# The sums of the adaLN modulation taken over 1024 columns and 128 rows at a time instead of 512 columns and 256 rows, and spread otherwise over the FFNs of a two-layer trunk

## The chip, the core and the metric

The kernel runs on one core of a Trainium2 chip. The metric is the device time of one execution in microseconds (us). Times are compared with those of the kernel before on the same chip.

## What is computed

A trunk of two layers over 512 positions of width 1024, all in float32. Layer 0 has a short gated convolution as its mixer, layer 1 a Mamba-2 SSD mixer; each is followed by a SwiGLU FFN (1024 to 2 x 2816 and back). What matters here is the modulation: a matrix of 1024 x 12288 is multiplied by one vector, and its 12288 results are twelve vectors of 1024, three for each of the four sub-layers.

```python
mod = (jax.nn.silu(c) @ ada_w + ada_b).reshape(bsz, DEPTH, 2, 3, D_MODEL)
for i in range(DEPTH):
    shift, scale, gate = (mod[:, i, 0, k][:, None, :] for k in range(3))
    h = rmsnorm(x, norm_g[i, 0]) * (1.0 + scale) + shift
    y = short_conv_mixer(h, ...) if i == 0 else ssd_mixer(h, ...)
    x = x + gate * rmsnorm(y, norm_g[i, 1])
    shift, scale, gate = (mod[:, i, 1, k][:, None, :] for k in range(3))
    h = rmsnorm(x, norm_g[i, 2]) * (1.0 + scale) + shift
    gate_, up = jnp.split(h @ f_w_in[i], 2, axis=-1)
    x = x + gate * rmsnorm((jax.nn.silu(gate_) * up) @ f_w_out[i], norm_g[i, 3])
```

`ada_w` is 1024 x 12288 (50 MB) and is read once. Each of its numbers is used once, so it is bound to transfers and to the engine that sums, not to matrix work.

## The kernel before

**Products.** TensorE (PE) multiplies float32 operands that are split in two halves of less precision, a high and a low one. ScalarE (ACT) rounds a staged weight tile to the high half (a CAST), and VectorE (DVE) subtracts it from the tile, which leaves the low half: this pair is called a split (L230 and L231 for tiles `wst`, L616 and L617 for tiles `wsu`). SyncE (SP) issues the loads of the weights, in the order of the program; the loads that add into a tile (`wsu<-wsu`) are issued by GpSimd (POOL).

**The order.** All of it is written out by hand: each engine gets its instructions in the order in which the program's lines come, and waits in that order. Python generators let one stage's steps be taken inside another's loop (`next(madds)`, `next(late, None)`).

**The FFNs.** The first product of each FFN (h times the 5632 columns of `f_w_in`) has two parts. Some columns go through a fast scheme with seven products per block instead of eight (a Strassen-Winograd scheme): its unit `u` takes 256 columns and issues seven groups of twelve matmuls of 256 columns, P1, P5, P2, P6, P3 for unit u and P7, P4 for the unit before, in the order P1, P7, P5, P2, P4, P6, P3. `fetch` loads a unit's weights two units ahead; `split_x`, `split_z`, `split_y`, `split_s` split them (L617); `c11`, `c12`, `c22`, `c21` combine the banks of PSUM (the memory that PE writes to) into results (L668, L672, L681, L687 to L689). In even units `c12` ends with a Silu on ACT. P4 adds into the bank that `c22` reads, and so waits for it, as `P6` waits for a copy that ACT makes of its bank (`keep`, L664). The first FFN has six such units, the second more. The rest of the columns go in plain chunks of 128 columns, 24 matmuls of 512 columns each (L285 to L287), the weights split two chunks ahead. After them comes the second factor (L1310 in the first FFN), whose weights `w2x` are split at L1282.

`Values` makes the other operand of the fast scheme from h: `sums`, `four` (two subtractions, L729), and `hi` and `lo`, which split the results (ACT L709, DVE L714).

**The modulation.** The first 16 blocks of 128 columns are done at the start by PE. All the rest is summed on DVE: `ada_load` (L997 in the loop of the first layer) brings a piece of `ada_w` into a tile `ada_st`, one of three; `ada_madd` multiplies it by a column of `csil`, which is silu(c), and adds it to `ada_acc` (L125 for the first piece, L127 for the others); `ada_fold` (L140) adds up groups of 32 partitions by a transposing reduction; `ada_fin` finishes with one small matmul (L147, `ada_ps`) and small additions on DVE (L151, L156). One load is 256 rows x 512 columns, two halves of 128 rows; so two sums of 128x512 are made from it, and a vector of 1024 needs two `ada_acc` and 16 sums. `sums(n)` takes n steps, one sum each, and a new load is issued after every second one.

In the mixer of layer 0 two to four sums stand in each chunk. In the units of the first FFN there are two, one behind `c11` and one at the end of the unit; three are ahead of the units, beside `four`. In the plain chunks that follow there are three or four in each.

The last of the twelve vectors is made inside the second FFN's units by `gate_late`, called `late`. It takes one step per unit, behind `c11`: in unit 0 it issues its first load, in unit 1 the second (L2247), and from unit 2 on it makes two sums per step, and then `ada_fin`.

Of the kernel before, what the change touches and what calls it, by code (L numbers as in the profile page):

```python
# [38 lines left out]
def trunk_kernel(  # L39
# [141 lines left out]
    def ada_first(j, i, staged, cpad):  # L181


        acc = ada_p[0].tile([P, 2, P], F32, tag="acc", name="ada0", bufs=2)
# [509 lines left out]
    class Values:  # L694
# [31 lines left out]

        def four(self, b):
            vb, k, (lo, hi) = self.vb[b], self.half[b], HALVES
            dve.tensor_tensor(vb[:, :, lo], vb[:, :, hi], vb[:, :, lo], SUB)  # L729
            self.hi(3, vb[:, :, lo], k)  # L730
            self.lo(3, vb[:, :, lo], k)
# [7 lines left out]
    ada_sets = []  # L739
    for q0 in (16, 0 + 24, 8 + 24, 16 + 24, 48, 56, 64, 72, 80):  # L740
        ada_sets += [q0 * P, q0 * P + 512]
# [4 lines left out]
    with ExitStack() as ph:  # L746
# [4 lines left out]
        four = gx.tile([P, P], F32, tag="four", name="four", bufs=1)  # L751
        make_four(four)
# [103 lines left out]
        with tc.manual_schedule(engines={PE_ENGINE, mybir.EngineType.SP, mybir.EngineType.Activation,  # L856
# [126 lines left out]
            def ada_begin(n):  # L983
                quarters.extend((c0, kh) for c0 in ada_sets[:n] for kh in range(4))
# [8 lines left out]
            def ada_load():  # L993
                if quarters:
                    c0, kh = quarters.pop(0)
                    st = ada_tile()
                    dma(st, ada_w[kh * 256:(kh + 1) * 256, c0:c0 + 512].rearrange("(k p) f -> p k f", p=P))  # L997
                    ada_st.append((c0, kh, st))

            def ada_steps():  # L1000
                n = 0
                while ada_st:
                    c0, kh, st = ada_st.pop(0)
                    if kh == 0:
                        acc = ada_p[0].tile([P, 512], F32, tag="acc", name="ada_acc", bufs=2)
                        if n % 2 == 0:
                            part = gx.tile([P, 32], F32, tag="fold", name="fold", bufs=2)
                    for k in range(2):
                        ada_madd(acc, st[:, k, :], kh * 2 + k)
                        if k:  # L1010
                            ada_load()
                            if kh == 3:
                                ada_fold(acc, part[:, n % 2 * 16:n % 2 * 16 + 16])
                                if n % 2:
                                    fins.append(ada_fin(c0 - 512, part, mm_ps if len(fins) == 2 else aux_ps))
                                n += 1
                        yield
# [40 lines left out]
            madds = ada_begin(6)  # L1058
# [13 lines left out]
            for k in range(18):  # L1072
# [20 lines left out]
                for _ in range((3, 4, 3, 2, 2, 2)[i]):  # L1093
# [241 lines left out]
        with tc.manual_schedule(engines={PE_ENGINE, mybir.EngineType.SP, mybir.EngineType.Activation,  # L1335
# [6 lines left out]
            madds = ada_begin(12)  # L1342
# [34 lines left out]
            sums(1)  # L1377
            acc.append(in_chunk(more[1], h))
            part_of.sum_s(0)
            part_of.split_s(0)  # L1380
            up(2, acc[0])
            vs.four(0)
            sums(2)
# [4 lines left out]
            for u in range(UN1):  # L1388
# [9 lines left out]
                if u:  # L1398
                    un.c12(v)
                else:  # L1400
                    vs.four(1)
# [14 lines left out]
                sums(1)  # L1416
# [17 lines left out]
                sums(1)  # L1434
# [15 lines left out]
            sums(3)  # L1450
# [6 lines left out]
            sums(2)  # L1457
# [4 lines left out]
            sums(4)  # L1462
# [16 lines left out]
            for k in range(k0, last + 1):  # L1479
# [17 lines left out]
                sums(3 if j == 3 else 4)  # L1497
# [577 lines left out]
    with ExitStack() as ph:  # L2075
# [137 lines left out]
        with tc.manual_schedule(engines={PE_ENGINE, mybir.EngineType.SP, mybir.EngineType.Activation,  # L2213
# [19 lines left out]
            four = s1t[:, 8, 0:P]  # L2233
            make_four(four)

            def gate_late():

                st = [raw[:, 18 + 2 * b:20 + 2 * b, :] for b in range(2)]
                acc = s1t[:, 9:11, :].rearrange("p a b -> p (a b)")
                part = s1t[:, 8, P:P + 32]  # L2240
                quarter = [(n, kh) for n in range(2) for kh in range(4)]

                def load(i):
                    if i < len(quarter):
                        n, kh = quarter[i]
                        c0 = 88 * P + n * T
                        dma(st[i % 2], ada_w[kh * 256:(kh + 1) * 256, c0:c0 + T].rearrange("(k p) f -> p k f", p=P))  # L2247

                load(0)
                yield  # L2250
# [283 lines left out]
```

## Time and the profile before

| | |
|---|---|
| median of 3 runs | 1344.95 us (1341.88 to 1347.98) |
| the profiled execution | 1345.36 us |
| its span in the trace | 1343.5 us |
| mean granted clock of TensorE | 0.995 |
| units of the first FFN | 253.48 to 319.79 us |
| its plain chunks | 319.79 to 455.01 us |
| from there to the second factor's first matmul | 457.36 (adaLN's), 458.46 (second factor's) |
| units of the second FFN | 1044.64 to 1206.5 us |
| adaLN's loads in the first layer's stages | 88 of 512 KB, 6.2 us from issue to landing |

In the profile, a line number is one of the kernel above, and helpers such as `product` or `split` give all their instructions one line, so that places are told apart by their time in the span. `x12` behind an operation is a group of twelve such instructions in a row. A bracket `[2.22 <-ACT g L664]` at the end of a timeline's row is the time that the engine stood idle ahead of it, and the instruction that it waited for. In rows of waits, the time in all, the number of waits and the longest stand behind the colon. Engines wait in their own order: an instruction that isn't ready holds all behind it on its engine. `SPq` and `PEq` are the sequencers that issue, `PEld` the loading of weights into TensorE beside its matmuls.

### The profile page before, as it was taken

The page shows a single profiled execution, that of the slowest core. Times are in us where ns is not written, and L with a number is a line of the kernel's source. Part 1 is how long each engine was busy: PE and PEld are TensorE (multiplying, and loading weights), DVE is VectorE, ACT ScalarE, POOL GpSimd, SP SyncE. Part 2 cuts the span into 40 slices and gives each one's busy share as a digit, 9 for nine tenths or more (in the row PEclk, how much of TensorE's full clock was granted, in tenths as well). Part 3 has the DMA queues.
Part 4 walks back from the last instruction along what each step waited for, and adds up shares of the span by engine and source line. Part 5 has one row for each costly group of instructions (what it writes and reads, how often), then busy time and mean ns, then how long its engine had stood idle before and what let it go on. Part 6 is the DMA issues. An engine that isn't in the chain of part 4 may idle for free.

```text
span 1343.5 us, 19889 instructions
## 1 busy us (share of the span) xinstructions
PE 1319.2 (98%) x7653; PEld 1145.6 (85%) x7653; DVE 1065.7 (79%) x1717; ACT 662.6 (49%) x1084; POOL 99.7 (7%) x123
## 2 busy tenths in 40 slices
PE   8999999999999899999999999999999999999998
PEld 7788889898888678898888888888789999998886
DVE  5588867786787897768999898888687788876888
ACT  5323355354122366565655555554474455454665
POOL 0000000010000140000000000000001111100330
PEclk9999999999999999999999999999999999999999
DMA  9757752587798982613542434323251999868871
GB/s 304 235 185 227 253 180 56 136 232 215 248 310 265 294 145 60 176 29 119 156 136 72 138 110 141 110 94 110 94 149 44 238 242 247 211 167 289 187 135 63
DMA packets 219939, 228.54 MB, mean 170 GB/s; under 512 B 9396, under 2 KB 163908, under 8 KB 218820
## 3 DMA queue, kind: packets, MB, share of 16 engines
q1 hardware_dynamic: 201248, 187.88, 45.3%
q0 software_dynamic: 14448, 26.48, 11.4%
q10 hardware_dynamic: 4148, 12.90, 3.0%
q8 instruction: 60, 0.98, 0.3%
q14 instruction: 35, 0.29, 0.1%
HBM read 198.52 MB, written 2.24 MB: 149 GB/s over the span
## 4 chain that ended last, share of the span: by engine, by line
PE 76%; DVE 11%; DMA 7%; ACT 3%; issue 2%; SPq 2%; DVEq 0%; ACTq 0%; POOLq 0%
PE y L387 10%; PE ip L285 9%; PE ip L287 9%; PE ip L286 9%; PE sA L654 6%; PE cA L2210 4%; DMA ada_st<-in_ada_w_dram 3%; PE sC L654 3%; PE cA L1310 3%; DVE ada_acc L127 2%; DMA wsu<-wsu 2%; PE li L285 2%; PE li L287 2%; PE li L286 2%; PE li L929 1%
## 5 line engine op out<-in xcount | busy, mean ns | idle before, releaser
L285 PE MATMUL ip<-h,whl 128*128 128x512 f32 x744 | 293.7, 395 | 0.2 <-DVE cv L1036 0.2
L287 PE MATMUL ip<-h,whl 128*128 128x512 f32 x744 | 289.9, 390 | 0.0
L286 PE MATMUL ip<-h,whl 128*128 128x512 f32 x744 | 289.6, 389 | 0.0
L285 PEld LDWEIGHTS ip<-h,whl 128*128 128x128 f32 x744 | 139.7, 188 | 29.9 <-issue 1.8
L287 PEld LDWEIGHTS ip<-h,whl 128*128 128x128 f32 x744 | 139.6, 188 | 29.9 <-DVE whl L231 0.4
L286 PEld LDWEIGHTS ip<-h,whl 128*128 128x128 f32 x744 | 139.8, 188 | 28.0
L231 DVE TENSOR_TENSOR whl<-wst,whl 128x1024 fp32r<-128x1024 f32 x86 | 104.3, 1219 | 29.2 <-ACT whl L230 29.2
L654 PE MATMUL sA<-tq,whl 128*128 128x256 f32 x792 | 104.3, 285 | 7.0 <-DVE g L681 4.0
L654 PEld LDWEIGHTS sA<-tq,whl 128*128 128x128 f32 x792 | 98.6, 192 | 10.0 <-DVE g L681 5.7
L230 ACT CAST whl<-wst 128x1024 fp32r<-128x1024 f32 x86 | 89.2, 1042 | 31.0 <-DMA wst<-in_f_w_in_dram 14.7
L127 DVE SCALAR_TENSOR_TENSOR ada_acc<-ada_st,csil,ada_acc 128x512 f32<-128x512 f32 x126 | 94.4, 749 | 11.8 <-DMA ada_st<-in_ada_w_dram 9.2
L387 PE MATMUL y<-whlo,ys 128*128 128x512 f32 x384 | 89.3, 392 | 0.0
L387 PEld LDWEIGHTS y<-whlo,ys 128*128 128x128 f32 x384 | 71.7, 188 | 15.9 <-issue 0.7
L285 PE MATMUL li<-h,whl 128*128 128x256 f32 x288 | 83.2, 289 | 0.0
L287 PE MATMUL li<-h,whl 128*128 128x256 f32 x288 | 81.5, 283 | 0.0
L286 PE MATMUL li<-h,whl 128*128 128x256 f32 x288 | 81.5, 283 | 0.0
L617 DVE TENSOR_TENSOR whl<-wsu,whl 128x1024 fp32r<-128x1024 f32 x46 | 56.1, 1220 | 24.9 <-ACT whl L616 24.7
L1673 DVE SCALAR_TENSOR_TENSOR cu<-ip,cols,cu 128x511 f32<-128x511 f32 (+2 forms) x84 | 62.8, 747 | 3.9 <-ACT cu L1670 1.4
L2210 PE MATMUL cA<-whlo,ao 128*128 128x512 f32 x264 | 61.0, 390 | 0.4 <-DVE c L2447 0.2
L2210 PEld LDWEIGHTS cA<-whlo,ao 128*128 128x128 f32 x264 | 49.3, 188 | 11.5 <-ACT whlo L2175 1.2
L285 PEld LDWEIGHTS li<-h,whl 128*128 128x128 f32 x288 | 55.2, 192 | 0.0
L286 PEld LDWEIGHTS li<-h,whl 128*128 128x128 f32 x288 | 55.2, 192 | 0.0
(383 smaller groups left out, 2509.8 us busy)
## 6 DMA issues: line engine op xcount, KB each, us to landing
ada_st<-in_ada_w_dram SPq DMA_DIRECT2D x88, 512.0 KB, 6.2
wst<-in_f_w_in_dram SPq DMA_DIRECT2D x18, 1024.0 KB, 7.7
wst<-in_m_w_in_dram SPq DMA_DIRECT2D x14, 1024.0 KB, 5.4
wsu<-in_f_w_in_dram SPq DMA_DIRECT2D x24, 512.0 KB, 5.8
sg<-in_f_w_in_dram SPq DMA_DIRECT2D x44, 256.0 KB, 3.9
wsu<-in_f_w_in_dram SPq DMA_DIRECT2D x44, 256.0 KB, 4.1
wst<-in_m_w_in_dram SPq DMA_DIRECT2D x20, 512.0 KB, 5.2
wst<-in_a_w_in_dram SPq DMA_DIRECT2D x9, 1024.0 KB, 7.3
```

The costliest lines, as they stand in the source:

```text
L127: dve.scalar_tensor_tensor(acc, w, csil[:, k:k + 1], acc, MUL, ADD)
L230: later.append((lambda sw=sw, w=w: act.copy(w[:, 0, :nk, :], sw), lambda sw=sw, w=w: dve.tensor_tensor(w[:, 1, :nk, :], sw, w[:, 0, :nk, : ...
L231: lambda sw=sw, w=w: dve.tensor_tensor(w[:, 1, :nk, :], sw, w[:, 0, :nk, :].bitcast(F32), SUB)))
L285: pe.matmul(dst, w_at(w, 0, kk), a[:, 0, sl], start=start, stop=False)
L286: pe.matmul(dst, w_at(w, 0, kk), a[:, 1, sl], start=False, stop=False)
L287: pe.matmul(dst, w_at(w, 1, kk), a[:, 0, sl], start=False, stop=stop)
L387: pe.matmul(pst, a[:, al, tk], wt[:, wl, kk, :], start=k == 0 and i == 0, stop=k == K - 1 and i == 2, skip_group_check=bool(held))
L617: dve.tensor_tensor(dst[:, 1], src, dst[:, 0].bitcast(F32), SUB)
L654: pe.matmul(dst, w[:, wl, k0 + k, :], self.moving(q, k, al), skip_group_check=True, start=q in self.FIRST and k == 0 and i == 0, stop=k == ...
L1310: pe.matmul(bank[r, sub], a[:, al, q, tk], w[:, wl, q, :], start=first and k == 0, stop=False, skip_group_check=True)
L1673: dve.scalar_tensor_tensor(u[:, sft:], pst[:, :T - sft], w[3 - sft], u[:, sft:], MUL, ADD)
L2210: pe.matmul(bank[r][sub], a[:, al, q, tk], w[:, hl, q, :], start=first and k == 0, stop=last and k == 2, skip_group_check=True)
```

## The change

A load of the modulation is now 128 rows x 1024 columns, as many bytes as before, and one sum of 128x1024 is made from it. There is one `ada_acc` of 1024 columns, and a vector of 1024 needs eight sums. A step of `sums` is one such sum, with one load issued behind it. The steps are spread otherwise: 2, 2, 1, 1, 1, 1 in the mixer's chunks; none ahead of the units of the first FFN and none in its unit 0; one in each of units 1 to 5, behind `c12`; eight between the units and the loop of plain chunks (2, 3, 3, where there were 3, 2, 4 half ones), and beyond that two per chunk (three in one). Both `four` of the first FFN's `Values` come as one, `fours`, ahead of unit 0: both subtractions, then both `hi`, then both `lo`. In the second FFN `late` takes its step behind `c12` and not in unit 0; its first step, in unit 1, issues two loads, makes the first sum and issues a third load, and each further step makes one sum.

```diff
+        def fours(self):
+            lo, hi = HALVES
+            for vb in self.vb:
+                dve.tensor_tensor(vb[:, :, lo], vb[:, :, hi], vb[:, :, lo], SUB)
+            for do in (self.hi, self.lo):
+                for vb, k in zip(self.vb, self.half):
+                    do(3, vb[:, :, lo], k)
...
-        ada_sets += [q0 * P, q0 * P + 512]
+    ada_sets = [q0 * P for q0 in (16, 24, 32, 40, 48, 56, 64, 72, 80)]
...
+        ada_acc = ada_p[0].tile([P, D], F32, tag="acc", name="ada_acc", bufs=1)
...
-                    dma(st, ada_w[kh * 256:(kh + 1) * 256, c0:c0 + 512].rearrange("(k p) f -> p k f", p=P))
+                    dma(st.rearrange("p a b -> p (a b)"), ada_w[k * P:(k + 1) * P, c0:c0 + D])
...
             def ada_steps():
                 while ada_st:
...
+                    c0, k, st = ada_st.pop(0)
+                    ada_madd(ada_acc, st.rearrange("p a b -> p (a b)"), k)
+                    ada_load()
+                    if k == KD - 1:
+                        part = gx.tile([P, 32], F32, tag="fold", name="fold", bufs=2)
+                        ada_fold(ada_acc, part)
+                        fins.append(ada_fin(c0, part, mm_ps if len(fins) == 2 else aux_ps))
+                    yield
...
-                for _ in range((3, 4, 3, 2, 2, 2)[i]):
+                for _ in range((2, 2, 1, 1, 1, 1)[i]):
                     next(madds)
...
             up(1, lead_ps[3])
-            sums(1)
             acc.append(in_chunk(more[1], h))
             part_of.sum_s(0)
             part_of.split_s(0)
+            vs.fours()
             up(2, acc[0])
-            vs.four(0)
-            sums(2)
...
                 un.product(u, "P1")
                 if u:
                     un.c12(v)
+                    sums(1)
                 else:
-                    vs.four(1)
                     up(3, acc[1])
...
                 un.c11(u)
-                sums(1)
                 un.split_z(u)
...
                     un.split_s(u + 1)
-                sums(1)
...
-            sums(3)
+            sums(2)
...
-            sums(2)
+            sums(3)
...
-            sums(4)
+            sums(3)
...
-                sums(3 if j == 3 else 4)
+                sums(3 if k == k0 + 6 else 2)
...
                 load(0)
-                yield
                 load(1)
-                for i, (n, kh) in enumerate(quarter):
+                for k in range(KD):
+                    ada_madd(acc, st[k % 2], k)
+                    load(k + 2)
+                    if k == KD - 1:
+                        ada_fold(acc, part)
                     yield
...
                     c12(v)
+                    next(late, None)
...
                 c11(u)
-                next(late, None)
```

The first place is DVE's order ahead of the first FFN's unit 0 and up to its unit 0's `c11` (L668). `raw_2192` holds the operand of `four`, `tq` its low halves, `raw_2193<-ip,g` is a product of a gate and an up half of the plain chunks ahead. Before:

```order
L637 TENSOR_TENSOR wsu<-sg,wsu 128x512
L617 TENSOR_TENSOR wss<-wsu,wss 128x512
L1197 TENSOR_TENSOR raw_2193<-ip,g 128x512
L729 TENSOR_TENSOR raw_2192<-raw_2192 128x2x256
L714 TENSOR_TENSOR tq_2187<-raw_2192,tq_2187 128x512
L127 SCALAR_TENSOR_TENSOR ada_acc<-ada_st,csil,ada_acc 128x512 x2
L729 TENSOR_TENSOR raw_2192<-raw_2192 128x2x256
L714 TENSOR_TENSOR tq_2187<-raw_2192,tq_2187 128x512
L1197 TENSOR_TENSOR raw_2193<-ip,g 128x512
L617 TENSOR_TENSOR whl<-wsu,whl 128x1024
L1191 TENSOR_TENSOR s1t<-raw_2193 128x512
L668 TENSOR_TENSOR g<-sB,g 128x256
```

And of the change (its L730 is L729 of before, its L1196 is L1197, its L1190 is L1191):

```order
L637 TENSOR_TENSOR wsu<-sg,wsu 128x512
L617 TENSOR_TENSOR wss<-wsu,wss 128x512
L730 TENSOR_TENSOR raw_2152<-raw_2152 128x2x256 x2
L714 TENSOR_TENSOR tq_2147<-raw_2152,tq_2147 128x512 x2
L1196 TENSOR_TENSOR raw_2153<-ip,g 128x512 x2
L617 TENSOR_TENSOR whl<-wsu,whl 128x1024
L1190 TENSOR_TENSOR s1t<-raw_2153 128x512
L668 TENSOR_TENSOR g<-sB,g 128x256
```

The two sums between the subtractions are gone, the subtractions stand together, and the two products of L1197 stand behind them.

The second place is DVE's order at the end of the first FFN's plain chunks, up to the first split of the second factor (`whlo<-w2x`). Before:

```order
L140 TENSOR_REDUCE fold<-ada_acc 128x16
L125 TENSOR_SCALAR ada_acc<-ada_st,csil 128x512
L151 TENSOR_TENSOR mods<-ada_ps,cols_92 32x8 x4
L231 TENSOR_TENSOR whl<-wst,whl 128x1024
L127 SCALAR_TENSOR_TENSOR ada_acc<-ada_st,csil,ada_acc 128x512 x7
L140 TENSOR_REDUCE fold<-ada_acc 128x16
L1282 TENSOR_TENSOR whlo<-w2x,whlo 128x1024
```

And of the change (its L1200, L1202 and L1281 are L1201, L1203 and L1282 of before):

```order
L127 SCALAR_TENSOR_TENSOR ada_acc<-ada_st,csil,ada_acc 128x1024 x2
L140 TENSOR_REDUCE fold<-ada_acc 128x32
L1200 TENSOR_TENSOR g<-ip,g 128x512
L231 TENSOR_TENSOR whl<-wst,whl 128x1024
L1202 TENSOR_TENSOR ff_3738<-g,ff_3738 128x512
L231 TENSOR_TENSOR whl<-wst,whl 128x1024
L151 TENSOR_TENSOR mods<-ada_ps,cols_92 32x8 x4
L156 SCALAR_TENSOR_TENSOR acol<-mods,cols_91 128x8
L1281 TENSOR_TENSOR whlo<-w2x,whlo 128x1024
```

The last fold now stands two weight splits ahead of the first split of the second factor, where it stood directly ahead of it.

The third place is the second FFN's unit 1, on DVE; `s1t<-raw,csil` is the first sum of `late`. Before:

```order
L617 TENSOR_TENSOR wss<-wsu,wss 128x512
L672 TENSOR_TENSOR g<-sC,g 128x256
L617 TENSOR_TENSOR whl<-wsu,whl 128x1024
L681 SCALAR_TENSOR_TENSOR g<-sA,g 128x256
L2134 TENSOR_TENSOR s1t<-raw 128x512
```

And of the change (its L2129 is L2134 of before):

```order
L617 TENSOR_TENSOR wss<-wsu,wss 128x512
L672 TENSOR_TENSOR g<-sC,g 128x256
L125 TENSOR_SCALAR s1t<-raw,csil 128x1024
L617 TENSOR_TENSOR whl<-wsu,whl 128x1024
L681 SCALAR_TENSOR_TENSOR g<-sA,g 128x256
L2129 TENSOR_TENSOR s1t<-raw 128x512
```

The first sum now stands between `c12` (L672) and the split of X (L617), with `c22` (L681) behind both. On SP, the loads of `late` and of the units' weights stand so in the change (before, one load `raw<-in_ada_w_dram` stood behind each unit's five loads of weights, beginning one unit earlier):

```order
L605 DMA wsu<-in_f_w_in_dram 128x4x128
L606 DMA wsu<-in_f_w_in_dram 128x8x128
L608 DMA wsu<-in_f_w_in_dram 128x4x128
L2239 DMA raw<-in_ada_w_dram 128x1024 x3
L602 DMA sg<-in_f_w_in_dram 128x4x128
L603 DMA sg<-in_f_w_in_dram 128x4x128
```

The first three loads of `late` now stand together, behind the fetch that unit 1 issues.

53 lines of the change are left out of this document (13 added, 40 removed).

## The prediction

> **What bounds the kernel now.** I read the page's busy times first, then TensorE's own waits, and then windows cut at the places where it waits.
>
> ```profile
> PE 1319.2 (98%) x7653; PEld 1145.6 (85%) x7653; DVE 1065.7 (79%) x1717; ACT 662.6 (49%) x1084; POOL 99.7 (7%) x123
> PE sA L654 <- DVE g L681: 4.0, 6, 1.3
> PE sA L654 <- ACT g L664: 2.5, 2, 2.2
> PE ada_ps L147 <- DVE fold L140: 2.2, 1, 2.2
> 253.48:319.79 66.31, 60.64 (x482) 59.42 (x481) 52.91 (x77) 31.93 (x54) 7.79 (x9) 0.97 0.82 215
> 319.79:455.01 135.22, 135.21 (x613) 111.86 (x611) 105.82 (x160) 32.72 (x41) 0.00 (x0) 1.00 0.83 270
> 455.01:476.89 21.88, 16.20 (x52) 11.40 (x52) 20.14 (x31) 10.21 (x15) 6.91 (x8) 0.84 1.02 268
> 1061.18 1.44 PE sC L654 x12
> 477.06 10.90 PE cB L1310 x48
> ```
>
> TensorE (PE) has work for 1319 of 1343.5 us, so VectorE's (DVE's) time counts only where PE waits for it. (Windows: stretch, length, then busy PE, PEld, DVE, ACT, POOL with counts, clock, DMA share, GB/s.) Two places stand out, and DVE is on both. At full rate twelve 256-wide matmuls take 1.44 us and a 512-wide one 10.90/48 = 0.227. The six units of the first FFN issue 40 groups of twelve: 40 x 1.44 = 57.6, but they take 66.31. **8.7 us are lost there.** From the end of its first product to the second factor of the next, 48 wide matmuls need 10.9 us and some 0.3 for two small ones, but take 21.88. **10.7 us are lost there.** Between the two PE is full.
>
> **Price of a sum.** What one half sum, one wide operation and one wide first sum take:
>
> ```profile
> L127 DVE SCALAR_TENSOR_TENSOR ada_acc<-ada_st,csil,ada_acc 128x512 f32<-128x512 f32 x126 | 94.4, 749 | 11.8 <-DMA ada_st<-in_ada_w_dram 9.2
> L231 DVE TENSOR_TENSOR whl<-wst,whl 128x1024 fp32r<-128x1024 f32 x86 | 104.3, 1219 | 29.2 <-ACT whl L230 29.2
> L213 DVE TENSOR_TENSOR whl<-wst,whl 128x512 fp32r<-128x512 f32 x36 | 22.6, 687 | 8.4 <-ACT whl L212 8.3
> L815 DVE TENSOR_SCALAR xn<-x,ss 128x1024 f32<-128x1024 f32 x2 | 1.5, 754 | 0.1
> ```
>
> No sum of 1024 columns with an addition is in this trace. Doubling 512 costs 1.219 - 0.687 = 0.532, so I take 0.749 + 0.532 = 1.28 us, against 1.50 for two halves: 0.22 saved per pair. Bounds: 1.22 (the wide row) to 1.50. Over 72 pairs that is about 16 us of DVE, all but a part of it beside PE's work. The bytes and the count of loads stay; only their rows become 4 KB instead of 2 KB.
>
> **First FFN's units: -7.3.** Unit 0 and unit 1:
>
> ```profile
> 256.11 1.53 DVE L127 SCALAR_TENSOR_TENSOR ada_acc<-ada_st,csil,ada_acc 128x512 f32<-128x512 f32 x2
> 258.28 0.63 ACT L709 ACTIVATE tq<-raw 128x512 fp32r<-128x512 f32 x1 [2.81 <-DVE raw L729]
> 259.75 0.36 ACT L664 COPY g<-sA 128x256 f32<-128x256 f32 x1
> 260.17 1.93 PE L654 MATMUL sA<-tq,whl 128*128 128x256 f32 x12 [2.22 <-ACT g L664]
> 262.00:264.00 2.00, 2.00 (x11) 2.00 (x11) 2.00 (x3) 0.00 (x0) 0.88 (x1) 0.50 1.14 289
> 267.69 0.74 DVE L127 SCALAR_TENSOR_TENSOR ada_acc<-ada_st,csil,ada_acc 128x512 f32<-128x512 f32 x1
> 268.35 0.42 DVE L672 TENSOR_TENSOR g<-sC,g 128x256 f32<-128x256 f32 x1
> 269.33 1.03 ACT L616 CAST whl<-wsu 128x1024 fp32r<-128x1024 f32 x1
> 270.40 1.23 DVE L617 TENSOR_TENSOR whl<-wsu,whl 128x1024 fp32r<-128x1024 f32 x1 [1.63 <-ACT whl L616]
> 271.54 0.42 DVE L681 SCALAR_TENSOR_TENSOR g<-sA,g 128x256 f32<-128x256 f32 x1
> 272.01 3.14 PE L654 MATMUL sA<-tq,whl 128*128 128x256 f32 x24 [1.20 <-DVE g L681]
> ```
>
> In unit 0, two sums on DVE (256.11) stand ahead of the subtraction (L729) that ScalarE (ACT) waits 2.81 us for, and the copy that frees PE (259.75) is queued behind that on ACT. The change takes all sums out of unit 0 and does both subtractions earlier; some 3.2 us of work (one sum of 0.48, two of 0.77, the two products of L1197) no longer stands ahead of the second one, so the wait of 2.22 goes. So does what followed it: the clock fell to 0.50, and the next four groups took until 267.77 instead of 265.93, 1.84 us. The Trainium skill (TensorE: Matmul & The Clock Gate, Part 1) lets the clock fall after at least one idle window of about 3.4 us; this gap of 2.22 sufficed, so the row decides; by the page the slow groups would have another cause, and this term would be 1.84 smaller.
>
> In unit 1 DVE does a sum (267.69), then c12 (L672), then idles 1.63 us while ACT computes Silu and the cast; after them come the split of X (L617) and c22 (L681), which PE waits for. The wide sum of 1.28 now lies in that hole of 1.63: it costs nothing there, and c12 comes 0.66 earlier. In odd-numbered products there is no Silu and no hole, and the sum delays the split by 1.28, but two half sums (1.5) ahead of it are gone. I keep one wait of about 1.1 us in unit 1, where c12 follows the long row of splits, and 0.3 for PE's refill: 8.7 - 1.4 = 7.3. Bounds: 4.1 (only unit 0's wait and clock) to 8.7.
>
> **The chunks between: +1.7.** Here DVE splits weights two chunks ahead, and late in the stretch it is hardly ahead:
>
> ```profile
> DVE ada_acc L127 <- DMA ada_st<-in_ada_w_dram: 9.2, 5, 4.3
> 419.88 1.23 DVE L231 TENSOR_TENSOR whl<-wst,whl 128x1024 fp32r<-128x1024 f32 x1 [1.64 <-ACT whl L230]
> ```
>
> The split that ends at 421.1 is for a chunk which starts near 421.8 (six chunks of 24 x 0.227 before 455.01): 0.7 us to spare. From 319.79 to there DVE has now 28 tiles to sum (7.5 were done before, 35.5 are done there), 28 x 2 x 0.77 = 43 us. After the change it is 35 tiles (5 before, 40 there), as ten are pulled ahead of the chunk loop and two in each chunk: 35 x 1.31 = 46 us with the gap of 0.03 to the next. That is 2.4 later, so PE waits about 1.7, once. Bounds: 0 (the waits for loads, 9.2 in all, shrink by 2) to 6.7 (they grow by 5). The eight tiles left are done three chunks before the end, so DVE catches up.
>
> **End of the first product: -10.0.**
>
> ```profile
> 455.02 1.54 DVE L127 SCALAR_TENSOR_TENSOR ada_acc<-ada_st,csil,ada_acc 128x512 f32<-128x512 f32 x2 [1.78 <-DMA ada_st<-in_ada_w_dram]
> 456.59 0.71 DVE L140 TRANSPOSE_TENSOR_REDUCE fold<-ada_acc 128x16 f32<-128x512 f32 x1
> 457.23 1.18 DVE L1282 TENSOR_TENSOR whlo<-w2x,whlo 128x1024 fp32r<-128x1024 f32 x1
> 457.36 0.41 PE L147 MATMUL ada_ps<-fold,four 128*128 128x32 f32 x2 [2.18 <-DVE fold L140]
> 458.46 10.79 PE L1310 MATMUL cA<-whlo,ao 128*128 128x512 f32 x35 [0.35 <-DVE whlo L1282]
> ```
>
> The last two sums wait for their load, the fold follows, and both the adaLN product on PE and the first split of the second factor (L1282) stand behind it. PE stops for 2.18 us, runs 35 matmuls in 10.79 instead of 7.9, and waits twice more for operands that are late for the same reason. Now the last sum lies about three chunks ahead, and the first split follows the last weight split: seven half sums, a wait and a fold (some 7.7 us) leave its front. The next product takes 2.7 us of PE per item, and DVE needs 1.2 + 0.7 + 0.7 = 2.6, so the lead holds. I leave 0.7 of the 10.7. Bounds: 5 to 10.7.
>
> **Second FFN's units: +9.0, less 0.8.** Here the change adds a wait.
>
> ```profile
> 1054.37 0.42 DVE L672 TENSOR_TENSOR g<-sC,g 128x256 f32<-128x256 f32 x1
> 1056.42 1.23 DVE L617 TENSOR_TENSOR whl<-wsu,whl 128x1024 fp32r<-128x1024 f32 x1 [1.63 <-ACT whl L616]
> 1056.99 1.19 SPq L2247 DMA_DIRECT2D raw<-in_ada_w_dram  x1
> 1058.04 3.14 PE L654 MATMUL sA<-tq,whl 128*128 128x256 f32 x24 [0.28 <-DVE g L681]
> DMA to landing us min/median/max: 5.1/5.9/7.1
> DMA to landing us min/median/max: 3.7/5.6/8.6
> PE sA L654 <- DVE g L681: 0.9, 3, 0.3
> ```
>
> (The two landing rows are those of L2247 and of L997, the same load in the first FFN; the last row is PE's wait from 1030 to 1230.) gate_late's first step loaded one tile in unit 0 and one in unit 1, and summed from unit 2 on. Now its first step, in unit 1, issues the first load and at once sums that tile. In SyncE's (SP's) order the load stands behind unit 3's five weight loads, as the one at 1056.99 does. So it lands at 1056.99 + 5.9 = 1062.9, and from 1054.8 DVE stands at the sum; queued behind are X's split and c22, for which PE waits. c22 then ends at 1062.9 + 0.75 + 1.14 + 0.42 = 1065.2, and PE goes on 7.2 us after 1058.04. A gap of over 7 us also halves the clock, 1.84 as in the first FFN: 9.0. Bounds: 5.0 (landing 3.7, no clock loss) to 11 (8.6). The median of the line itself is the nearest row. [...] From unit 2 on a tile has a whole unit to land. Of the remaining waits (0.9 in three, each with a refill of 0.26) I let 0.8 go, as the two half sums behind c11 leave; the fold in unit 8 may take it back.
>
> **Sum.** The profiled execution took 1345.36 (span 1343.5 and 1.9 around it), 0.4 above the median of the three, 1344.95. -7.3 + 1.7 - 10.0 + 9.0 - 0.8 = -7.4, so **1338.0 us**.
>
> **Rivals.**
> 1. **Transfers, not DVE, pace the first FFN's units.**
>
> ```profile
> 298.03 6.97 DMA wsu<-wsu
> ```
>
> The accumulating transfers (7 us) lie on the chain that ended last, and each fetch waits for one. Against it: at 257 us fetch 2 stood behind an adaLN load which waited for a sum, and without it that chain starts over 4 us earlier. Then only unit 0's 4.1 are gained, and perhaps 1 less at the other places: 1341 to 1344. Chance 0.19.
>
> 2. **The late load costs little**, because it lands after 3.7 and the clock stays up: 9.0 becomes 5.0, 1334. The order on SP speaks against. Chance 0.09.
>
> 3. **Slower: loads can't feed two tiles per chunk.** Three buffers at two tiles per 5.45 us give each 8.2 us a turn; less its own sum of 1.3, a load has 6.9 us to land. The median of 5.6 is under that, the longest of 8.6 over. From a usual landing of about 7 us, DVE stays late through the whole stretch: 6.7 instead of 1.7 there, and at its end the 10.0 are not gained. 1345.4 - 7.3 + 6.7 + 9.0 - 0.8 = 1353. Chance 0.14.
>
> **How the numbers follow.** The forecast has 0.58, with a range of its own of 1334 to 1342; the limit of 0.5% (what a measurement can tell here), 1338.2, cuts it in half. Faster: 0.29 + 0.09 + 0.02 (of the first rival) = 0.40; same 0.29 + 0.17 = 0.46; slower 0.14. The range 1332 to 1346.5 holds all but the third rival and the outer ends of the terms.
>
> **What would show it.** After: no wait of PE for L664 near 258, one of about 1 us in unit 1, a full clock to 476; no wait for the fold at the end of the first product; a sum of about 1.28 us; and in the second FFN's unit 1 a first sum (L125) that waits some 8 us for a load, PE idle some 7 us behind it and a granted clock of 0.50 after. I am wrong if that load has landed by 1055, if PE still waits at the end of the first product, or if the chunks lose over 5 us.

## The result, and the profile after

The changed kernel takes **1347.56 us** (median of 20 runs, 1344.6 to 1351.46); the kernel before, on the same chips, 1345.67 (20 runs, 1341.88 to 1348.67). The ratio is 1.0012, with a 95% interval of 1.0003 to 1.0021: 0.12% slower, well inside the 0.5% that the prediction takes as the limit of what a measurement can tell here. The forecast was 1338.0, between 1332 and 1346.5. So the expected gain of some 7 us is missing, and another 2 are lost: 9.5 us lie between the forecast and the measured time.

Windows of the changed kernel, cut as before (units of the first FFN; its plain chunks; the first 48 matmuls of the second factor; units of the second FFN):

```profile
252.78:312.51 59.73, 58.50 (x481) 57.79 (x480) 48.65 (x66) 30.58 (x52) 7.82 (x9) 1.00 0.80 208
312.51:457.10 144.59, 137.31 (x615) 111.80 (x614) 109.90 (x133) 37.38 (x48) 0.00 (x0) 1.00 0.82 275
457.10:468.30 11.20, 11.20 (x51) 9.18 (x50) 9.89 (x15) 6.74 (x10) 4.30 (x5) 1.00 1.05 279
1036.10:1208.30 172.20, 161.70 (x1322) 161.27 (x1321) 129.26 (x179) 85.24 (x144) 25.01 (x29) 0.97 0.81 207
```

and the last of these of the kernel before:

```profile
1044.64:1206.24 161.60, 160.24 (x1322) 158.79 (x1321) 130.36 (x188) 84.81 (x144) 25.14 (x29) 1.00 0.86 221
```

The start of the units comes 0.70 earlier (252.78 against 253.48). Then: units 66.31 to 59.73, **-6.58**; plain chunks 135.22 to 144.59, **+9.37**; first block of the second factor 21.88 to 11.20, **-10.68**; second FFN's units 161.60 to 172.20, **+10.60**. All between and behind these differs by 0.1. The sum, +2.1, is the difference of the spans, 1343.5 and 1345.6. The first FFN's units and the first block are near their sizes in the forecast (-7.3, -10.0), the second FFN's units are 2.4 above theirs (+8.2), and the plain chunks, with +1.7 there, are 7.7 off.

What TensorE waits for in the changed kernel, whole span, and what DVE waits for in the plain chunks (L125 is the first sum of each vector, L127 the others):

```profile
PE sA L654 <- DVE g L681: 9.8, 3, 8.6
PE ip L287 <- DVE whl L231: 5.6, 6, 1.5
PE sA L654 <- DVE raw L681: 1.9, 1, 1.9
PE ip L285 <- ACT whl L230: 1.6, 2, 1.1
DVE ada_acc L127 <- DMA ada_st<-in_ada_w_dram: 18.5, 10, 6.4
DVE ada_acc L125 <- DMA ada_st<-in_ada_w_dram: 0.6, 1, 0.6
```

And of the kernel before, TensorE's waits in the second factor's first block, and DVE's from 319.79 to 457, up to the first split of the second factor:

```profile
PE cA L1310 <- ACT ao L1290: 1.7, 1, 1.7
PE cA L1310 <- DVE ao L1291: 1.3, 1, 1.3
DVE ada_acc L127 <- DMA ada_st<-in_ada_w_dram: 8.9, 4, 4.3
DVE ada_acc L125 <- DMA ada_st<-in_ada_w_dram: 3.2, 1, 3.2
```

The waits of before for the fold (L147, 2.2), for the second factor's operands and for ACT's copy in unit 0 (L664, 2.2) are gone. New are eight waits in the plain chunks, for the weights' splits (L231) and casts (L230), and in the second FFN one of 8.6 us and one of 1.9. DVE's waits for `ada_w` were 12.1 us in 5 and are 19.1 in 11.

The plain chunks in detail. What SP issues: the three loads of 1 MB of `w2x`, and around the second of them a weight pair and two loads of `ada_w`:

```profile
344.00 1.11 SPq L1234 DMA_DIRECT2D w2x<-in_f_w_out_dram  x1
...
367.75 0.43 SPq L221 DMA_DIRECT2D wst<-in_f_w_in_dram  x1
368.22 0.84 SPq L1234 DMA_DIRECT2D w2x<-in_f_w_out_dram  x1
...
374.88 8.04 SPq L1004 DMA_DIRECT2D ada_st<-in_ada_w_dram  x2
...
394.71 1.10 SPq L1234 DMA_DIRECT2D w2x<-in_f_w_out_dram  x1
```

DVE's three longest waits, the split behind the second of them, and then the matmul that waits for that split:

```profile
356.07 1.28 DVE L127 SCALAR_TENSOR_TENSOR ada_acc<-ada_st,csil,ada_acc 128x1024 f32<-128x1024 f32 x1 [4.35 <-DMA ada_st<-in_ada_w_dram]
...
381.28 1.28 DVE L127 SCALAR_TENSOR_TENSOR ada_acc<-ada_st,csil,ada_acc 128x1024 f32<-128x1024 f32 x1 [6.43 <-DMA ada_st<-in_ada_w_dram]
382.48 1.22 DVE L231 TENSOR_TENSOR whl<-wst,whl 128x1024 fp32r<-128x1024 f32 x1
...
406.09 1.28 DVE L127 SCALAR_TENSOR_TENSOR ada_acc<-ada_st,csil,ada_acc 128x1024 f32<-128x1024 f32 x1 [3.67 <-DMA ada_st<-in_ada_w_dram]
```

```profile
383.76 0.50 PE L287 MATMUL ip<-h,whl 128*128 128x512 f32 x1 [1.49 <-DVE whl L231]
```

The three waits end 11 to 13 us after a load of `w2x` was issued, which is about when it lands. From issue to landing took, first for `w2x`, then for `ada_w` in this stage:

```profile
DMA to landing us min/median/max: 11.7/11.7/11.7
DMA to landing us min/median/max: 3.7/5.9/8.6
```

The chunk with three sums (they start at 383.62, 384.9 and 386.95) comes behind the first two of the three waits, so it did not make these. Behind the one at 381 stands the split of a chunk's weights (382.48), and TensorE waits for it. SP then stands too: its next loads of `ada_w` (374.88, 8.04 us for two) wait for buffers, and the next weights wait behind them.

### The profile page after: what moved, and what is told of

Its sections match the earlier page's. It is cut to its first block, busy times and chain, and to the rows that moved or that the text cites. A ratio compares the mean times of both kernels' runs of the same rounds, so it can differ in the third digit from the quotient of the medians.

```text
span 1345.6 us, 19807 instructions
## 1 busy us (share of the span) xinstructions
PE 1314.5 (98%) x7653; PEld 1143.0 (85%) x7653; DVE 1049.8 (78%) x1627; ACT 662.6 (49%) x1084; POOL 99.5 (7%) x123
## 4 chain that ended last, share of the span: by engine, by line
PE 82%; DMA 8%; DVE 5%; SPq 2%; ACT 2%; issue 2%; DVEq 0%; ACTq 0%; POOLq 0%
PE ip L285 10%; PE ip L287 10%; PE ip L286 10%; PE y L387 10%; PE sA L654 8%; DMA ada_st<-in_ada_w_dram 5%; PE cA L2205 4%; PE sC L654 4%; PE cA L1309 3%; PE li L285 2%; PE li L287 2%; PE li L286 2%; PE sB L654 2%; DVE ada_acc L127 2%; PE li L936 1%
## 5 line engine op out<-in xcount | busy, mean ns | idle before, releaser
L231 DVE TENSOR_TENSOR whl<-wst,whl 128x1024 fp32r<-128x1024 f32 x86 | 104.4, 1219 | 31.3 <-ACT whl L230 31.3
L654 PE MATMUL sA<-tq,whl 128*128 128x256 f32 x792 | 106.0, 289 | 11.7 <-DVE g L681 9.8
L230 ACT CAST whl<-wst 128x1024 fp32r<-128x1024 f32 x86 | 89.2, 1042 | 48.6 <-DMA wst<-in_f_w_in_dram 46.4
L127 DVE SCALAR_TENSOR_TENSOR ada_acc<-ada_st,csil,ada_acc 128x1024 f32<-128x1024 f32 x63 | 80.7, 1281 | 19.6 <-DMA ada_st<-in_ada_w_dram 19.1
L617 DVE TENSOR_TENSOR whl<-wsu,whl 128x1024 fp32r<-128x1024 f32 x46 | 56.2, 1222 | 25.0 <-ACT whl L616 25.0
L285 PEld LDWEIGHTS li<-h,whl 128*128 128x128 f32 x288 | 55.3, 192 | 0.0
L1228 POOL DMA_DIRECT2D sg<-sg x22 | 19.1, 870 | 488.5 <-DMA sg<-in_f_w_in_dram 287.9
```

The lines of the kernel that those rows point to most:

```text
L127: dve.scalar_tensor_tensor(acc, w, csil[:, k:k + 1], acc, MUL, ADD)
L230: later.append((lambda sw=sw, w=w: act.copy(w[:, 0, :nk, :], sw), lambda sw=sw, w=w: dve.tensor_tensor(w[:, 1, :nk, :], sw, w[:, 0, :nk, : ...
L231: lambda sw=sw, w=w: dve.tensor_tensor(w[:, 1, :nk, :], sw, w[:, 0, :nk, :].bitcast(F32), SUB)))
L285: pe.matmul(dst, w_at(w, 0, kk), a[:, 0, sl], start=start, stop=False)
L617: dve.tensor_tensor(dst[:, 1], src, dst[:, 0].bitcast(F32), SUB)
L654: pe.matmul(dst, w[:, wl, k0 + k, :], self.moving(q, k, al), skip_group_check=True, start=q in self.FIRST and k == 0 and i == 0, stop=k == ...
```

## The experiments

**Which place costs what.** First the second FFN, put right alone.

```diff
                 load(0)
+                yield
                 load(1)
+                yield
                 for k in range(KD):
...
                 else:
+                    next(late, None)
                     t_four(1)
```

> The changed kernel, but gate_late issues its first load in unit 0 of the second FFN and its second in unit 1, and makes its first sum in unit 2 (the sums stay 128x1024 wide and behind c12). Theory (the loss of the second FFN is the wait of DVE for a load that was only just issued): the wait of 9.3 us at L125 and PE's wait of 8.6 behind it go, the units of the second FFN take about 163 to 164 us instead of 172.3, and the whole is 8 to 10 us faster than the change, near 1338.5. Rival (the wide sum behind c12 itself delays c22 in every odd unit): most of the loss stays, the units take over 168.

It took 1339.28 us, 0.9958 of before (0.9938 to 0.9978). The units of the second FFN took 164.1 us, not 172.2: 8.1 of the 10.6 are the late load. In the other 2.5 lie smaller waits: 3.7 us in six, the longest 1.1, where the kernel before has 1.3 in five. The plain chunks stayed at 143.7.

Then three kernels on the plain chunks. In the first every load of `ada_w` there serves two sums, so that half of these pieces are left out and the modulation is another one:

```diff
                     ada_st.append((c0, k, st))
+                    if len(quarters) < 41 and len(ada_sets) == 0 and k < KD - 1:
+                        c0, k = quarters.pop(0)
+                        ada_st.append((c0, k, st))
...
-                    ada_load()
+                    if not any(s is st for _, _, s in ada_st):
+                        ada_load()
```

> The changed kernel, but in the first FFN's plain chunks each piece of ada_w is used for two sums, so that 20 of the 40 loads there are left out, while all sums stay. Theory T1 (the loads, with three buffers and the weights' loads behind them on SP, hold DVE up): the stage from 312.5 goes from 144.6 back to about 135.5 us, and the whole is 8 to 10 us faster than the change. Rival T2 (DVE's own work of 40 wide sums between the splits makes the splits late): the stage stays over 141, the gain is under 3.

In the second the sums are half as wide, and what the other half of the columns would add is left out:

```diff
-                    ada_madd(ada_acc, st.rearrange("p a b -> p (a b)"), k)
+                    narrow = not ada_sets and k
+                    ada_madd(ada_acc[:, 0:512] if narrow else ada_acc, st[:, 0, :] if narrow else st.rearrange("p a b -> p (a b)"), k)
```

> The changed kernel, but the sums of the last six vectors after the first piece of each take only the first 512 of their 1024 columns; all loads stay. This takes some 0.53 us from each of about 35 sums in the plain chunks. T1: the loads still come as late and DVE waits the longer for them; the stage stays over 140, the gain is 1 to 4. T2: the stage goes back to about 136, the gain is 8 to 10.

Windows of the plain chunks, first with half the loads, then with narrow sums; behind each the row of DVE's waits for `ada_w`:

```profile
312.39:447.40 135.01, 135.01 (x615) 112.23 (x614) 110.49 (x133) 37.69 (x48) 0.00 (x0) 1.00 0.68 218
DVE ada_acc L125 <- DMA ada_st<-in_ada_w_dram: 0.4, 1, 0.4
```

```profile
313.10:450.50 137.40, 135.72 (x615) 112.08 (x613) 89.78 (x133) 37.26 (x48) 0.00 (x0) 1.00 0.85 287
DVE ada_acc L127 <- DMA ada_st<-in_ada_w_dram: 28.4, 13, 6.4
```

With half the loads the stage is full: 135.01, all of it busy on PE, with DVE at 110.49 as in the changed kernel (109.90). So DVE's work alone does not make the splits late, and T2 as it stood falls. But narrow sums bring 7.2 us too, which T1 did not expect: 20 us of DVE's work go, its waits for loads grow by 10, and 7.2 of the rest are gained. The two lie on one chain: a load waits for a buffer, the buffer for its sum, the sum for the splits ahead of it, and those for weights that stand behind loads of `ada_w` on SP. What is taken off at the loads or at the sums helps, in whole or in part; the last link is tried next. The whole took 1338.56 (0.9944, 0.9926 to 0.9962) and 1339.51 (0.9957, 0.9941 to 0.9972).

In the third the weights go ahead of two of the loads on SP:

```diff
-                if k % 2 == 0 and k + 4 <= last:
+                if k == k0:
                     load_pair_at(k + 4)
...
                 low_parts()
+                if k % 2 and k + 5 <= last:
+                    load_pair_at(k + 5)
                 sums(3 if k == k0 + 6 else 2)
```

> The changed kernel, but in the first FFN's plain chunks each weight pair is loaded ahead of the sums of the chunk before, not behind them, so two loads of ada_w fewer stand ahead of it on SP. If the weights' place on SP behind loads that wait for buffers is what costs: the stage goes from 144.6 to 138 or less. If DVE is late because it waits for its own loads of ada_w (18.5 us in all) and the splits queue behind these: the stage stays at 142 to 146, since loads of ada_w then come still later.

1349.23 us (1.0025, 1.0005 to 1.0045), the stage at 144.6: nothing is gained by the weights' place. ACT's waits for them fell from 46.4 to 18.7 us, while DVE's for `ada_w` stayed (18.7 at L127, which had 18.5). So taking off the last link alone gains nothing.

**The form and the placement apart.** The kernel before with wide loads and sums, one sum where the first of two half sums stood:

```diff
+                    ada_madd(ada_acc, st.rearrange("p a b -> p (a b)"), k)
+                    ada_load()
...
                     yield
+                    yield
```

> The kernel before with the form of the sums alone changed: loads of 128 rows x 1024 columns, one wide sum per load, taken where the first of its two half sums stood, nothing placed otherwise, and the second FFN as before. Theory: the form frees about 0.2 us of DVE per pair of half sums beside TensorE's work and moves the second half sum's 0.75 ahead; the two places where TensorE waits stay (the first FFN's units 65 to 67 us, the end of the first product 17 to 20 us from the second factor's first matmul to its second block), and the time stays within 3 us of before. Rival: the form itself (4 KB rows, one accumulator) carries a gain or a loss: over 5 us either way.

1335.69 us, **0.9936 of before (0.9917 to 0.9955)**: the rival was right, the form by itself brings 9 us. Its plain chunks, the second factor's first block, and the first split of the second factor:

```profile
318.58:453.40 134.82, 134.82 (x613) 112.05 (x612) 103.18 (x122) 34.00 (x45) 0.00 (x0) 1.00 0.83 279
453.40:466.00 12.60, 11.37 (x53) 9.03 (x52) 11.98 (x21) 8.20 (x13) 5.16 (x6) 1.00 1.04 278
448.12 1.18 DVE L1274 TENSOR_TENSOR whlo<-w2x,whlo 128x1024 fp32r<-128x1024 f32 x1
```

From 318.58 to 466.00 are 147.4 us; before it was 135.22 + 21.88 = 157.1. The units took 65.2 and the second FFN's 161.6, about as before. The form takes off 0.2 us per pair, measured (1.282 for a wide sum against 2 x 0.749), some 35 times in this stage, 7 us. DVE starts the first split of the second factor 5.3 us ahead of the stage's end (448.12), where it was 2.2 behind it (457.23): 7.5 us. And that is the place where TensorE had waited for DVE. The rows of 4 KB may have a small part in it: DVE's waits for `ada_w` in the stage are 10.7 us here and were 12.1. Half sums from such loads weren't run in the old placement.

The same with the sum at the second of the two steps (the edit is against that run):

```diff
                 while ada_st:
+                    yield
                     c0, k, st = ada_st.pop(0)
...
                     yield
-                    yield
```

> As the run with the form alone changed (1335.7), but the wide sum stands where the second of the two half sums stood, not the first. If that run gained because DVE has 0.23 us less to do per pair: the time stays at 1334 to 1338, with the second factor's first block at 12 to 14 us. If it gained because a sum taken at once gives its buffer back a step earlier, so that the next load is issued earlier: 1340 to 1346, and the first block goes back to 16 to 19 us.

1337.75 us (0.9942, 0.9921 to 0.9964), first block 16.0. The time says DVE's work; the block is at the edge of what the other theory expected, since the last sums stand later. The 2 us between the two runs lie within their intervals, so the two don't tell whether an earlier return of the buffers is worth anything here.

And the new placement with two half sums per load:

```diff
-                    ada_madd(ada_acc, st.rearrange("p a b -> p (a b)"), k)
+                    for f in range(2):
+                        ada_madd(ada_acc[:, f * 512:f * 512 + 512], st[:, f, :], k)
```

> The changed kernel with its placement and its loads, but each wide sum as two half sums of 128x512 from the same load. It adds about 0.23 us of DVE to each of the 72 sums. If DVE's work is part of the closed chain in the plain chunks (two tiles per chunk): 35 x 0.23 = 8 us there and little elsewhere, the stage at 150 to 153 us, the whole 1353 to 1358. If only the landing of loads sets the pace: the stage stays under 147, the whole 1347 to 1350.

1348.56 us (1.0019, 1.0001 to 1.0037), the stage at 146.4. So in the new placement the form is worth 1 us, in the old one 9: where loads set the pace, DVE's saved work turns into longer waits for them (at L127 16.2 us here, 18.5 with wide sums).

**The first FFN's unit 0.** The two subtractions apart again, the sums still out of there:

```diff
-            vs.fours()
             up(2, acc[0])
+            vs.four(0)
...
                 else:
+                    vs.four(1)
                     up(3, acc[1])
```

> The changed kernel, but the two subtractions are apart again as before, the second in unit 0 of the first FFN; the sums stay out of there. If the two sums ahead of the second subtraction made the wait of before: the units stay at 59.7 to 61.5 us. If the place of the subtractions made it: a wait of 1.5 us or more for ACT's copy comes back in unit 0, with a lower clock behind it, and the units take over 63.

1348.23 us (1.0028, 1.0013 to 1.0043), units 60.9. Some 5.4 of the 6.6 us come from the absence of the sums there; the order of the subtractions gives 1.1 at most.

**Where the sums stand in the chunks.** Between the units and the loop stand ten sums (2, 2, 3 and 3; the section on the change says eight), the other 33 of the 43 in this stage in the loop. With the second FFN's loads early (that part of the edit is as shown above), the loop's sums over more chunks:

```diff
-                sums(3 if k == k0 + 6 else 2)
+                sums((1, 2, 2, 2, 1, 2, 2, 1, 1, 2, 2, 2, 1, 2, 2, 2, 2, 2, 2, 0)[k - k0])
```

> As the run with the second FFN's loads one unit early (1339.3), and the 33 sums of the loop of plain chunks go over 18 chunks and not 16.5: one in the chunk that loads w2x and in a few others, two elsewhere. Theory (a closed chain of three buffers, the sums and the splits runs at the limit where two tiles per chunk are asked for, above all behind the 1 MB loads of w2x): DVE's waits for ada_w fall, the stage goes from 144 to 139 to 142 us, the whole to 1335 to 1338. Rival (only the total number of loads and sums in the stage counts): the stage stays at 143 to 145, the whole at 1339.

1336.62 us (0.9947, 0.9931 to 0.9964). The table reaches into the nineteenth chunk, not the eighteenth as the text said. The stage went from 143.9 to 135.3 us (to the second factor's first matmul), more than expected. But the last sums and their fold stood in front of the second factor again, whose first block went from 11.0 us to 18.6; its waits:

```profile
PE cA L1309 <- ACT ao L1289: 2.7, 2, 1.7
PE cA L1309 <- DVE ao L1290: 1.3, 1, 1.3
```

So the table was drawn a chunk shorter:

```diff
+                sums((1, 2, 2, 2, 1, 2, 2, 2, 1, 2, 2, 2, 2, 2, 2, 2, 2, 2, 0, 0)[k - k0])
```

> As the run that spread the sums (its last two stood in the nineteenth chunk of the loop, and it lost 7.4 us at the second factor's first block), but the 33 sums end in the eighteenth: one in each of the three chunks that load w2x, two in the fifteen others. No sums ahead of the units. Theory (the stage stays full while no more than two tiles are asked for per chunk and fewer in those with w2x; the first block is full if the last fold stands a chunk earlier): the stage 135 to 137 us, the first block 10.8 to 12, the whole 1329 to 1333. Rival (two tiles in most chunks is already past the limit): the stage at 140 or more, the whole over 1335.

**1329.88 us, 0.988 of before (0.9863 to 0.9896).** Its plain chunks, first block, and DVE's waits for `ada_w` in them:

```profile
312.01:446.90 134.89, 134.89 (x613) 112.14 (x612) 106.86 (x125) 35.55 (x46) 0.00 (x0) 1.00 0.87 290
446.90:459.70 12.80, 11.55 (x52) 8.96 (x51) 12.19 (x21) 8.39 (x13) 4.42 (x6) 1.00 1.00 266
DVE ada_acc L127 <- DMA ada_st<-in_ada_w_dram: 9.3, 10, 3.0
```

With this table the plain chunks are full: 15 of the 18 chunks still take two tiles, and TensorE is never idle. The first block takes more than the 12 us that were expected at most; there TensorE waits once, 1.2 us, for an operand. Against the changed kernel one sum fewer stands in each of the three chunks that load `w2x` and in the one that had three; they come a chunk or two later. The longest wait for a load fell from 6.4 to 3.0 us. A pair of chunks, 10.9 us, with a weight pair, `w2x` and four tiles moves 4.2 MB, 385 GB/s, where the changed kernel's mean in the stage was 275; with one tile fewer 337. That is an estimate from the sizes. The highest rate that this run shows over such a stretch is about the same, with the DMA engines full (a share of 1.06):

```profile
350.15:361.05 10.90, 10.90 (x51) 9.04 (x50) 8.84 (x16) 2.66 (x3) 0.00 (x0) 1.00 1.06 392
```

So a pair of chunks with `w2x` and four tiles leaves nothing over to catch up with. How the gain divides between the chunks with `w2x`, the chunk with three sums and the longer table wasn't tried apart.

**Three sums ahead of the units.** (Of this edit only the new places are shown, of the next all but the second FFN's part.)

```diff
+            sums(1)
             vs.lo(0, va[:, :, lo_])
+            sums(1)
             rest(1)
...
             vs.hi(2, va[:, :, hi_])
+            sums(1)
             vs.lo(2, va[:, :, hi_])
             part_of.fetch(1)
```

> As the run with the second FFN's loads one unit early, and three sums go ahead of the first FFN's units, to places between 225 and 250 us where DVE waits for ACT; the 30 sums of the loop go over 18 chunks; the second FFN's fold has a step of its own. Theory: 37 tiles instead of 40 are left for the stage, 3 x 2.2 us (a load's turn of 6.6 over three buffers, or a sum of 1.3 with its share of waits) fewer: the stage takes 136 to 139 us, the second FFN's units 163, the whole 1329 to 1334. Rival: three sums ahead of the units make TensorE wait at the boundary (over 1 us there), or the stage stays over 142.

1334.09 us (0.9923, 0.99 to 0.9947). The stage was full (135.1, block 11.0), and the boundary did not suffer, but the units took 64.4. The rows of SP, of ACT and of PE:

```profile
235.54 11.37 SPq L1004 DMA_DIRECT2D ada_st<-in_ada_w_dram  x3
246.96 0.43 SPq L602 DMA_DIRECT2D sg<-in_f_w_in_dram  x1
260.85 1.05 ACT L616 CAST whl<-wsu 128x1024 fp32r<-128x1024 f32 x1 [3.07 <-DMA wsu<-wsu]
265.28 2.93 PE L654 MATMUL sA<-tq,whl 128*128 128x256 f32 x12 [3.15 <-ACT g L664]
```

The third load waits for its sum until 246.5 and holds the fetch of unit 1 back on SP; the accumulating transfer comes late, and TensorE waits 3.15 us. This is what the first rival of the prediction speaks of, brought about by a load in the wrong place.

With two sums there, in the gap of 2.8 us, 31 in the loop, and the second FFN as in the kernel before:

```diff
+            sums(2)
             vs.lo(0, va[:, :, lo_])
...
+                sums((1, 2, 2, 2, 1, 2, 2, 2, 1, 2, 2, 1, 1, 2, 2, 2, 2, 2, 0, 0)[k - k0])
```

> The changed kernel with three places put otherwise: the second FFN as in the kernel before; two wide sums ahead of the first FFN's units, in the 2.8 us in which DVE waits for ACT near 235 us; the 31 sums left for the loop of plain chunks go over 18 chunks, at most two in each, one in those that load w2x and in two more. Theory (each loss found so far is one of placement): units of the first FFN 59 us, plain chunks 135 to 136, the second factor's first block 10.8, the second FFN's units 161.6: 252.8 + 59 + 135.5 + 10.8 + 568.5 + 161.6 + 137.2 = 1325.4 of span, 1327 in time. Rival (the two early sums or the denser loop cost what they did in the run with three): 1331 to 1335.

**1327.74 us, 0.987 of before (0.9845 to 0.9896)**, with every term as expected within 1.2 us. It is the fastest of all and beats both kernels:

```profile
252.92:313.12 60.20, 58.76 (x482) 57.84 (x481) 49.06 (x66) 30.54 (x52) 7.79 (x9) 1.00 0.82 210
313.12:447.90 134.78, 134.78 (x613) 112.05 (x612) 107.10 (x126) 37.89 (x48) 0.00 (x0) 1.00 0.85 286
447.90:459.00 11.10, 11.10 (x53) 9.20 (x52) 10.48 (x20) 6.75 (x10) 4.30 (x5) 1.00 1.07 285
1028.64:1190.40 161.76, 160.27 (x1323) 158.82 (x1322) 130.45 (x188) 84.78 (x144) 25.06 (x29) 1.00 0.86 221
```

The second FFN's units, with their half sums behind `c11` as before, take 3.0 us less here than with wide sums behind `c12` and early loads in the run with the shorter table (164.8).

## Why the prediction was wrong

**Units of the first FFN, -7.3: right**, -6.58. The wait for L664 in unit 0 and the low clock are gone, and two waits of 0.6 are left. The first rival (transfers pace the units) falls for this kernel. The 1.84 us for the clock are in part luck, since a gap such as the one of 2.22 does not always bring the clock down (last section).

**Plain chunks, +1.7: the step that failed.** They lost 9.37, more than the upper bound of 6.7, and over 5 was named as a sign of being wrong. The term was sized by DVE's work, 43 against 46 us, and took the waits for loads to stay as they were; the bound let them grow by 5. They grew by 7.0, from 12.1 to 19.1 us. (The 9.2 of the prediction is L127 alone and leaves out the wait of 3.2 at a vector's first sum; and by its own factors the work grows by 2.7, not by 2.4.) The 1.7 for the work and 7.0 for the waits are 8.7 of the 9.37, by estimate. The count of tiles per chunk was in the text, but the stage's transfers were never added up chunk by chunk, so that it did not show that three of the chunks also carry 1 MB of `w2x`. The third rival had the mechanism and 0.14: loads that cannot feed the chunks, 6.7 us. It was wrong in two points. Two tiles per chunk are not past the limit as such, since 15 of the 18 chunks take them in the run with the shorter table, where TensorE never waits. And the lateness does not reach the end: sums stop three chunks before it, and DVE catches up.

**End of the first product, -10.0: right**, -10.68. But either half of the change brings it: the form alone left 12.60 of the 21.88 us, the new placement with half sums 11.0. So this gain and that of the form can't be added.

**Second FFN, +9.0: right in the mechanism**, with two sizes off that nearly cancel. DVE's and PE's rows in unit 1:

```profile
1055.55 0.75 DVE L125 TENSOR_SCALAR s1t<-raw,csil 128x1024 f32<-128x1024 f32 x1 [9.30 <-DMA raw<-in_ada_w_dram]
1057.82 4.39 PE L654 MATMUL sA<-tq,whl 128*128 128x256 f32 x24 [8.61 <-DVE g L681]
```

and the window behind the gap:

```profile
1058.00:1060.00 2.00, 2.00 (x10) 2.00 (x11) 1.25 (x3) 1.43 (x3) 0.00 (x0) 0.50 0.68 252
```

The gap cost 8.61, and the 24 matmuls behind it 4.39 instead of 3.14, with a granted clock of 0.50: 9.9 us, less the 0.3 of before. The wait was forecast at 7.2, since the load was to land 5.9 us after its issue; it was issued at 1048.83 and had landed by 1055.55, 6.7 us later. The clock was forecast at 1.84 and cost 1.25. (The upper bound, with a landing after 8.6, comes to 11.7 by the same sum, not 11.)

**Its other waits, -0.8: wrong**, about +1. Those of before, 1.3 us in five, are gone, more than was let go. But in the unit with the last sum the fold follows it at once, and both stand ahead of the split that TensorE waits for:

```profile
1127.71 1.28 DVE L127 SCALAR_TENSOR_TENSOR s1t<-raw,csil,s1t 128x1024 f32<-128x1024 f32 x1
1129.03 1.25 DVE L140 TRANSPOSE_TENSOR_REDUCE s1t<-s1t 128x32 f32<-128x1024 f32 x1
1131.77 4.65 PE L654 MATMUL sA<-tq,whl 128*128 128x256 f32 x24 [1.89 <-DVE raw L681]
```

The gap is 1.89, and the slow matmuls behind it cost another 1.5. The prediction named the fold as what may take the 0.8 back, and did not price it.

**The price of a sum, 1.28: right** (1.282). But its effect was told as lying beside TensorE's work "all but a part". That part was the larger stake: in the old placement it is 9 us, as the form alone showed.

## What to carry to other kernels

When work with its own loads is moved, add up the bytes of each step where it lands, with the other loads of that step, and not only the engine's time: here a ring of three buffers, a queue and an engine that each go in order formed one chain, and a burst in one step held up what stood behind it. A change that bundles a cheaper form with a new placement should be run in two halves, since here the form gained some 9 us and the placement lost some 10. And a first step that issues a load and uses it at once puts the whole latency in front of everything queued behind it; issued one unit earlier, it made DVE wait for nothing.

## What the runs showed of the hardware

How long TensorE may idle before its clock falls does not follow from the length of the gap alone. A window behind the gap of 1.89 us in the changed kernel, and two gaps of the run with two half sums per load, each with the four microseconds behind it:

```profile
1134.00:1136.00 2.00, 2.00 (x12) 2.00 (x11) 1.59 (x3) 1.32 (x2) 0.00 (x0) 0.55 1.10 202
```

```profile
390.61 0.50 PE L287 MATMUL ip<-h,whl 128*128 128x512 f32 x1 [2.35 <-DVE whl L231]
390.61:394.61 4.00, 4.00 (x17) 3.30 (x18) 3.86 (x5) 1.37 (x2) 0.00 (x0) 1.00 0.60 180
410.05 0.79 PE L287 MATMUL ip<-h,whl 128*128 128x512 f32 x1 [2.38 <-DVE whl L231]
410.05:414.05 4.00, 4.00 (x11) 3.21 (x12) 3.29 (x5) 0.65 (x2) 0.00 (x0) 0.63 1.00 344
```

Behind 1.89 and 2.38 us the clock was down (means of 0.55 and 0.63 in the stretches shown), behind 2.35 it stayed full. A gap of 1.99 in the same place as the 1.89 also left it full in two other runs (the one with two half sums, and the one with the subtractions apart): their 24 matmuls took 3.13 and 3.14 us. The eight gaps of 3.1 us and more that the traces of these runs mark from 250 us on were all followed by a clock of 0.50 within two microseconds. The price does not grow with the gap: 24 matmuls took 4.65 us behind 1.89 and 4.39 behind 8.61. The Trainium skill (TensorE: Matmul & The Clock Gate, Part 1) speaks of an idle window of about 3.4 us; the clock also fell behind gaps shorter than that, and the rows decide here.
